# Fixed orders for VectorE, ScalarE and GpSimd, planned at build time from TensorE's order

## The chip, the cores and the metric

One core of a Trainium2 chip. The metric is the device time of one execution in microseconds. Before the change the median of three runs is 2024.77 (2024.56 to 2024.83).

## The reference

Two layers of a decoder trunk, 512 tokens of 1024 numbers, all float32. Cut to what matters:

```python
for l in range(2):
    h = rms_norm(x, gn[0])
    x = x + 0.5 * rms_norm(swiglu(h, w_ffn1_gate[l], w_ffn1_up[l], w_ffn1_down[l]), gn[1])   # D_FF 2816
    h = rms_norm(x, gn[2])
    hq, hf, hi, hg, aq, ak, av, gate_a, gate_b = split(h @ w_in[l])
    y_hg = hgrn2_mixer(hq, hf, hi, hg, ...) @ w_branch_hgrn[l]     # gated linear recurrence, 4 heads, RMS norm for each head
    y_at = swa_sink_attention(aq, ak, av, sinks) @ w_branch_attn[l]  # window 128, 8 heads, softmax with sinks
    x = x + rms_norm((sigmoid(gate_a) * y_hg + sigmoid(gate_b) * y_at) @ w_out[l], gn[3])
    h = rms_norm(x, gn[4])
    x = x + 0.5 * rms_norm(swiglu(h, w_ffn2_gate[l], w_ffn2_up[l], w_ffn2_down[l]), gn[5])
```

## The kernel before

Each large float32 product is three products of fp32r parts: an operand is split into a rounded part `hi` and the rest `lo`, and TensorE computes hi·hi + hi·lo + lo·hi (`mm3`). The split is work for the other engines. ScalarE rounds (`whi`, L288 and L359 for weights, L432 and L442 for activations), VectorE subtracts (`wlo`, L296 and L363; L433), and for some pieces ScalarE writes the negated value (L355, L443) and a GpSimd DMA adds the original onto it (L358, L444).

The FFNs use a scheme with seven products in place of eight. It needs sums and differences of weight quarters (VectorE L340 to L345 into `tt` tiles in the up and gate part, L264 in the down projection), of activations (`quarter_sums`, L490 to L497; for it `Pre.sums`, L595, first adds hi and lo), and of results (L968, L1063 to L1070). After each sub-layer stand two norms for each of four token tiles: squares with a running sum on ScalarE (L639), a root (L644 to L646), the residual step (L863), squares again, and the scaling (L874); then TensorE turns the tile (transposes, L126) and L624 and L630 split it for the next sub-layer.

In the mixer the recurrence's output of each head is normed: Square (L1289), sum (L1291), Sqrt (L1292), reciprocal (L1293), multiply (L1295). The attention beside it takes its exponentials at L1374. ScalarE holds the tables of one set of functions and loads another set where the function needs it (ACT_TABLE_LOAD). PSUM has eight banks, five `acc` and three `aux`; a product into a bank waits until the last reader of the bank's earlier contents is done.

TensorE's order is written out in the program, with coroutines (`Order`, L63) that put small products between the large ones after given delays (`WAIT`). The other engines' orders come from the framework's scheduler, which goes by its own costs; at some 40 places `pin` (`tc.keep_in_program_order`) holds an instruction where the program states it, and `hold` does so in some stretches. Weights come by SyncE's queue in the order of use into four buffers (`w32`), at L244 in four pieces for a 512 KB unit in the down projections, at L247 in one piece elsewhere; at L255 aside into `s` tiles. Each engine runs its own queue strictly in order, so what waits at its head holds back what stands behind.

Of the kernel before, what the change touches and what calls it, by code (L numbers as in the profile page):

```python
# [15 lines left out]
P = 128  # L16
D = 1024
S = 512
# [26 lines left out]

@with_exitstack
def trunk(ctx: ExitStack, tc: tile.TileContext, xin, wall, gains, lbT, hgain, sinks, c_dist, c_mask, c_ident, out):
# [12 lines left out]
    def nm(s):  # L60
        seq[0] += 1
        return f"{s}_{seq[0]}"

    def big(dt=F32, shape=None):
        return sb.tile(shape or [P, S], dt, tag="s", name=nm("s"), bufs=SLOTS)

    def small(shape, tag, bufs=4, dt=F32):
        return sb.tile(shape, dt, tag=tag, name=nm(tag), bufs=bufs)

    def acc():  # L70
        return ps.tile([P, S], F32, tag="acc", name=nm("acc"), bufs=5)

    def aux():
        return ps.tile([P, S], F32, tag="aux", name=nm("aux"), bufs=3)
# [73 lines left out]
    pin = tc.keep_in_program_order  # L148
# [10 lines left out]
    class Stream:  # L159
# [78 lines left out]
        def load(self, upto):  # L238
            while self.dma < min(upto, self.n):
                w = sb.tile([P, D], F32, tag="w32", name=nm("w32"), bufs=W32)  # L240
                u = self.dma
                if isinstance(self.src[u], list):
                    for c, a in self.src[u]:
                        nc.sync.dma_start(w.rearrange("p (m c) -> p m c", m=4) if c is None else w[:, c], a)  # L244
                else:
                    for c in (slice(0, D // 2), slice(D // 2, D)) if u == 0 else (slice(0, D),):
                        nc.sync.dma_start(w[:, c], wall[self.src[u]][:, c])  # L247
                self.raw[u] = w
                self.dma += 1
# [8 lines left out]
        def quarter(self, it):  # L258
# [27 lines left out]
            it.hi, it.lo = (sb.tile([P, D + 64], F32R, tag=t, name=nm(t), bufs=WS)[:, it.at : it.at + D] for t in ("whi", "wlo"))  # L286
# [28 lines left out]
        def hold(self, i):  # L315
            if self.tight:
                pin(i)
# [6 lines left out]
        def split(self):  # L324
# [5 lines left out]
            it.hi, it.lo = (sb.tile([P, D + 64], F32R, tag=t, name=nm(t), bufs=WS)[:, it.at : it.at + D] for t in ("whi", "wlo"))  # L330
# [6 lines left out]
            if it.kind == "b":  # L337

                self.t13 = sb.tile([P, D], F32, tag="tt", name=nm("tt"), bufs=2)
                pin(nc.vector.tensor_tensor(self.t13[:, h[0]], w[:, h[0]], v[:, h[0]], op=ALU.add))  # L340
                pin(nc.vector.tensor_tensor(self.t13[:, h[1]], v[:, h[0]], v[:, h[1]], op=ALU.add))  # L341
                self.t = t = sb.tile([P, D], F32, tag="tt", name=nm("tt"), bufs=2)
# [357 lines left out]
    def down(src, kt, l, n, nxt, fast):  # L700
# [31 lines left out]
        def fetch():  # L732
            g = sb.tile([P, D], F32, tag="tt", name=nm("grow"), bufs=2)
# [302 lines left out]
    def sevenths(pre, between=lambda: None, first=True):  # L1036
# [23 lines left out]
        m = sb.tile([P, 4, H2], F32, tag="m", name=nm("m"), bufs=1)  # L1060
# [82 lines left out]
    class Scores:  # L1143
# [38 lines left out]
        def before(self, b):  # L1182
            self.mv = mv = sb.tile([P, 2 * TT, 96], F32, tag="tt", name=nm("mv"), bufs=2)
# [468 lines left out]
```

## Time and profile before

| what | value |
|---|---|
| profiled execution, its own time | 2024.79 us |
| its span, first to last instruction | 2023.0 us |
| TensorE (PE), share of the span | 100%, 13553 instructions |
| weight loads (PEld) | 89% |
| VectorE (DVE) | 80%, 2894 instructions |
| ScalarE (ACT) | 63%, 2213 instructions |
| GpSimd (POOL) | 13%, 318 instructions |
| moved over the span | 328.07 MB, 162 GB/s |

The busy share of TensorE counts a matmul from its start to a modelled end, so that neighbours overlap; a hole between two matmuls is seen in the list of waits and in the start times of the timeline. A row of the timeline reads: start, duration, engine, line, operation, out<-in, shapes, count, and in brackets the idle time before it with what ended it. Several instructions of one kind in a row are merged, and their duration runs from the first start to the last end.

### The profile page before, as it was taken

How to read it: one execution, taken by the hardware profiler on the slowest of the kernel's cores; microseconds unless marked ns; L12 is line 12 of the kernel's file. 1: busy time of each engine (PE TensorE's matmuls, PEld its weight loads, DVE VectorE, ACT ScalarE, POOL GpSimd, SP SyncE). 2: the span in 40 equal slices, each digit the busy share in tenths (PEclk: the TensorE clock that was granted, in tenths of full speed). 3: DMA queues.
4: the chain of work that ended last, by engine and by line, in shares of the span. 5: the costliest groups of instructions: out<-in, count | busy, mean ns of one | idle time of the engine just before them, and what ended most of it. 6: DMA issues, size and time to landing. Idle time of an engine off the chain costs nothing.

```text
span 2023.0 us, 36425 instructions
## 1 busy us (share of the span) xinstructions
PE 2016.2 (100%) x13553; PEld 1809.1 (89%) x13553; DVE 1624.3 (80%) x2894; ACT 1265.2 (63%) x2213; POOL 268.3 (13%) x318
## 2 busy tenths in 40 slices
PE   9999999999999999999999999999999999999998
PEld 8899988877898999998899998898778989999987
DVE  5888899767786788888998888977686858888888
ACT  7566687447364566658766666864554646666684
POOL 0111140000000011113211111400000100111140
PEclk9999999999999999999999999999999999999999
DMA  8688798311246368879768888872122554788794
GB/s 257 159 193 198 177 203 244 109 63 64 83 104 208 112 158 190 193 189 208 202 170 196 196 190 203 189 223 86 61 74 63 151 182 123 170 193 200 175 202 122
DMA packets 166801, 328.07 MB, mean 162 GB/s; under 512 B 19072, under 2 KB 85088, under 8 KB 166624
## 3 DMA queue, kind: packets, MB, share of 16 engines
q1 hardware_dynamic: 122416, 228.16, 34.1%
q0 software_dynamic: 44064, 97.54, 28.5%
q8 instruction: 106, 1.74, 0.3%
q14 instruction: 71, 0.58, 0.1%
q10 hardware_dynamic: 144, 0.05, 0.0%
HBM read 213.43 MB, written 14.73 MB: 113 GB/s over the span
## 4 chain that ended last, share of the span: by engine, by line
PE 93%; DVE 3%; ACT 1%; DMA 1%; issue 1%; SPq 0%; DVEq 0%; ACTq 0%
PE acc L116 71%; PE aux L116 20%; PE aux L126 2%; DVE wlo L296 1%; DVE s L264 1%; DMA w<-wall 1%; PE acc L126 0%; ACT whi L288 0%; DVE s L968 0%; SPq L244 0%; ACT s L442 0%; ACT s L443 0%; DVE wlo L363 0%; DVE s L863 0%; DVE s L433 0%
## 5 line engine op out<-in xcount | busy, mean ns | idle before, releaser
L116 PE MATMUL acc<-s,whi 128*128 128x256 f32 (+1 forms) x4998 | 1018.9, 303 | 0.0
L116 PEld LDWEIGHTS acc<-s,whi 128*128 128x128 f32 x4998 | 791.5, 188 | 46.6 <-issue 3.2
L116 PE MATMUL acc<-s,wlo 128*128 128x256 f32 (+1 forms) x2488 | 752.5, 302 | 0.1
L116 PEld LDWEIGHTS acc<-s,wlo 128*128 128x128 f32 x2488 | 467.9, 188 | 23.3 <-DVE wlo L363 0.4
L116 PE MATMUL acc<-whi,s 128*128 128x512 f32 x1360 | 441.5, 393 | 0.0
L359 ACT CAST whi<-w 128x1024 fp32r<-128x1024 f32 (+1 forms) x310 | 286.1, 926 | 195.0 <-PE acc L116 124.5
L358 POOL DMA_DIRECT2D wlo<-w x178 | 154.6, 869 | 1200.2 <-ACT wlo L355 715.0
L116 PEld LDWEIGHTS acc<-whi,s 128*128 128x128 f32 x1360 | 255.3, 188 | 57.1 <-issue 3.2
L116 PE MATMUL acc<-wlo,s 128*128 128x512 f32 x680 | 265.5, 390 | 0.2 <-DVE wlo L296 0.2
L355 ACT ACTIVATE wlo<-w 128x1024 fp32r<-128x1024 f32 (+1 forms) x178 | 154.6, 869 | 137.1 <-PE aux L116 98.2
L116 PE MATMUL aux<-s,whi 128*128 128x256 f32 (+1 forms) x1296 | 226.9, 278 | 0.0
L359 ACT CAST whi<-tt 128x1024 fp32r<-128x1024 f32 x160 | 168.4, 1053 | 83.2 <-DVE tt L341 43.0
L363 DVE TENSOR_TENSOR wlo<-w,whi 128x1024 fp32r<-128x1024 f32 (+1 forms) x132 | 157.4, 1205 | 78.3 <-ACT whi L359 78.1
L363 DVE TENSOR_TENSOR wlo<-tt,whi 128x1024 fp32r<-128x1024 f32 x160 | 195.4, 1221 | 9.9 <-ACT whi L359 7.3
L116 PEld LDWEIGHTS aux<-s,whi 128*128 128x128 f32 x1296 | 195.8, 188 | 1.1 <-issue 0.5
L116 PE MATMUL aux<-s,wlo 128*128 128x256 f32 (+1 forms) x648 | 179.8, 277 | 0.0
L116 PEld LDWEIGHTS acc<-wlo,s 128*128 128x128 f32 x680 | 127.8, 188 | 27.0 <-DVE wlo L296 2.1
L116 PE MATMUL aux<-whi,s 128*128 128x512 f32 x432 | 143.7, 390 | 0.0
L444 POOL DMA_DIRECT2D s<-s x128 | 111.1, 967 | 223.5 <-ACT s L432 104.7
L116 PEld LDWEIGHTS aux<-s,wlo 128*128 128x128 f32 x648 | 121.6, 188 | 0.4
L296 DVE TENSOR_TENSOR wlo<-s,whi 128x512 fp32r<-128x512 f32 x160 | 102.7, 686 | 9.9 <-ACT whi L288 9.9
L1070 DVE TENSOR_TENSOR m<-aux,s 128x512 f32<-128x512 f32 x80 | 55.2, 690 | 52.0 <-PE aux L116 51.5
(184 smaller groups left out, 2485.1 us busy)
## 6 DMA issues: line engine op xcount, KB each, us to landing
w<-wall SPq DMA_DIRECT2D x267, 512.0 KB, 3.9
wlo<-w POOLq DMA_DIRECT2D x98, 512.0 KB, 5.4
w<-wall SPq DMA_DIRECT2D x224, 128.0 KB, 3.5
wlo<-w POOLq DMA_DIRECT2D x80, 256.0 KB, 4.2
s<-wall SPq DMA_DIRECT2D x128, 128.0 KB, 4.2
s<-s POOLq DMA_DIRECT2D x64, 256.0 KB, 4.6
x_d<-s SPq DMA_DIRECT2D x48, 256.0 KB, 4.7
s<-x_d SPq DMA_DIRECT2D x48, 256.0 KB, 5.1
```

What stands on the lines that cost most here:

```text
L116: nc.tensor.matmul(o, lhsT, rhs, start=start, stop=stop)
L126: nc.tensor.transpose(o, src, ident)
L264: pin(nc.vector.tensor_tensor(o[c], x[c], y[c], op=op))
L296: pin(nc.vector.tensor_tensor(it.lo[:, h[c]], w[c], it.hi[:, h[c]].bitcast(F32), op=ALU.subtract))
L355: i = nc.scalar.mul(it.lo[:, c], w[:, c], -1.0)
L358: nc.gpsimd.dma_start(it.lo[:, c].bitcast(F32), w[:, c], accum_op=ALU.add)
L359: i = nc.scalar.copy(it.hi[:, c], w[:, c])
L363: self.hold(nc.vector.tensor_tensor(it.lo[:, c], w[:, c], it.hi[:, c].bitcast(F32), op=ALU.subtract))
L444: nc.gpsimd.dma_start(lo.bitcast(F32), src, accum_op=ALU.add)
L1070: ws.hold(nc.vector.tensor_tensor(m[:, 1:3, :], pairs[2], v[:, ::-1, :], op=ALU.add))
```

## The change

All `pin` and `hold` calls become empty, so the program states no order for the three engines any more. At the end of the build `arrange` reads the finished instruction list. `Step` gives every instruction a duration and a time to its result from formulas; `graph` finds the dependences, those through reused buffers too; `ranks` works back from TensorE's order, run without a wait, to the latest time at which each instruction may end; `simulate` runs all queues and on each free engine starts, among what can start soonest (within 0.4 us), the one with the earliest such time. Twelve rounds of this raise the rank of what TensorE waited for, and the round with the earliest end wins. Its orders are fixed by dependences between neighbours. TensorE's order, the DMAs and all arithmetic stay. Tiles are made by one helper, `take`, that also notes the number of buffers; names that were given apart from the tag (`grow`, `mv`) are now `tt`.

```diff
+EARLY_NS, NEAR_NS, TABLE_NS, HOT_NS, SEM_NS = 8000.0, 400.0, 1280.0, 3000.0, 55.0
+ROUNDS = 12
...
+        if op == "InstDMACopy":
+            self.bytes, self.rate = 4 * m * P, 197.0 if i.engine == EN.Pool else 412.0
+            self.cost = 930.0 if i.engine == EN.Pool else 60.0
+            self.time = 2600.0 + self.bytes / self.rate
...
+        elif i.engine == EN.Activation:
+            self.cost = max(0.85 * m + 85.0, 190.0) + (100.0 if len(self.writes) > 1 else 0.0)
+            self.time = self.cost + 100.0 + SEM_NS
+        elif i.engine == EN.DVE:
+            one = op == "InstTensorScalarPtr" and not i.is_scalar_tensor_tensor
+            self.cost = 0.78 * m + 10.0 if one else 1.045 * m + 72.0
+            self.time = self.cost + 78.0 + SEM_NS
...
+def simulate(steps, tags, homes, turn, ideal, rank):
...
+        first = min(x[0] for x in c)
+        near = [x for x in c if x[0] <= first + NEAR_NS]
+        if e == EN.Activation and len(near) > 1:
+            hot = [x for x in near if rank[x[1].n] + lag < x[0] + HOT_NS]
+            near = hot or [x for x in near if x[1].table in (0, table)] or near
+        b = min(near, key=lambda v: (rank[v[1].n], v[1].n))
...
+        for o in s.after:
+            o.left -= 1
+            t = end if o.engine != e or s.bytes else x + s.cost
+            if t >= o.ready:
+                o.ready, o.cause = t, s
...
+    for _ in range(ROUNDS):
+        order = simulate(steps, tags, homes, turn, ideal, rank)
+        end = pe[-1].start
...
+    for l in best[1].values():
+        for a, b in zip(l, l[1:]):
+            tc.add_manual_dep(by[b], a, info, reason="arrange")
...
-    pin = tc.keep_in_program_order
+    def pin(i):
+        return i
...
         def hold(self, i):
-            if self.tight:
-                pin(i)
+            pass
...
+    arrange(nc, tc, homes)
```

Line numbers in the rows of the new orders are those of the new file, 314 or 315 more than before at these places. The number behind a name tells its buffers apart, and in both orders it stands for the same tile.

ScalarE at the head norms of layer 0's recurrence (about 454 us in the span). `s_5263` are the squares, `ss_5265` the sums under the root, `es_5300` and `den_5303` belong to the softmax. Before:

```order
L1289 ACTIVATE s_5263<-aux_5255 128x512
L1292 ACT_TABLE_LOAD
L1292 ACTIVATE ss_5265<-ss_5265,eps_t 128x4
L1369 ACT_TABLE_LOAD
L1369 ACTIVATE es_5300<-es_5300 128x8
L1396 COPY s_5287<-aux_5277 128x512
L1396 COPY s_5288<-aux_5278 128x512
L1374 ACTIVATE s_5187,den_5303<-s_5187,neg_5298 128x256 x2
```

After:

```order
L1603 ACTIVATE s_5263<-aux_5255 128x512
L1688 ACTIVATE s_5187,den_5303<-s_5187,neg_5298 128x256 x2
L1606 ACT_TABLE_LOAD
L1606 ACTIVATE ss_5265<-ss_5265,eps_t 128x4
L1688 ACT_TABLE_LOAD
L1688 ACTIVATE s_5191,den_5303<-s_5191,neg_5298 128x256
L1710 COPY s_5287<-aux_5277 128x512
L1710 COPY s_5288<-aux_5278 128x512
```

The two exponentials (a merged row, x2) that stood behind the copies now stand between the squares and the load of the table that the root needs, and the small exponential on `es_5300` moved away from here.

VectorE at the turn of layer 0's stream out of the mixer (about 693 us). L630 splits the turned tiles, L644, L646, L863 and L874 are the norm chain of the last token tile (`rt_7599` its second root, `s_7603` and `s_7604` its scaled halves), `wlo_7637` and `wlo_7667` are weight splits. Before:

```order
L646 RECIPROCAL rt_7586<-rt_7586 128x1
L863 SCALAR_TENSOR_TENSOR s_7305<-s_7333,rt_7586,s_7305 128x512
L863 SCALAR_TENSOR_TENSOR s_7307<-s_7584,rt_7586,s_7307 128x512
L644 TENSOR_SCALAR rt_7599<-ss_1393_7594 128x1
L646 RECIPROCAL rt_7599<-rt_7599 128x1
L874 TENSOR_SCALAR s_7603<-s_7305,rt_7599 128x512
L874 TENSOR_SCALAR s_7604<-s_7307,rt_7599 128x512
L363 TENSOR_TENSOR wlo_7637<-w_1333_7339,whi_7636 128x1024
L363 TENSOR_TENSOR wlo_7667<-w_1336_7345,whi_7666 128x1024
```

After:

```order
L677 TENSOR_TENSOR wlo_7637<-w_1333_7339,whi_7636 128x1024
L944 SCALAR_TENSOR_TENSOR s_7538<-aux_7532,g_sb,s_7537 128x256
L944 SCALAR_TENSOR_TENSOR s_7541<-aux_7532,g_sb,s_7540 128x256
L677 TENSOR_TENSOR wlo_7667<-w_1336_7345,whi_7666 128x1024
L958 TENSOR_SCALAR rt_7550<-ss_1381_7545 128x1
L958 TENSOR_SCALAR rt_7586<-ss_1322_7318 128x1
L960 RECIPROCAL rt_7550<-rt_7550 128x1
L1188 TENSOR_SCALAR s_7554<-s_7301,rt_7550 128x512
L1188 TENSOR_SCALAR s_7555<-s_7303,rt_7550 128x512
```

The two weight splits that stood behind the last L874 now stand ahead of the whole chain of the norm, whose first two instructions (`rt_7550`, `rt_7586`) follow them.

VectorE in a down projection of layer 0's second FFN (about 948 us). L264 adds weight quarters in `s` tiles, L296 writes the low part that TensorE reads. Before:

```order
L264 TENSOR_TENSOR s_10854<-s_10854,s_10714 128x512
L264 TENSOR_TENSOR s_10855<-s_10855,s_10715 128x512
L296 TENSOR_TENSOR wlo_10864<-s_10821,whi_10863 128x512
L296 TENSOR_TENSOR wlo_10864<-s_10822,whi_10863 128x512
L264 TENSOR_TENSOR s_10821<-w_1844_10376,s_10821 128x512
L264 TENSOR_TENSOR s_10822<-w_1844_10376,s_10822 128x512
L296 TENSOR_TENSOR wlo_10891<-s_10854,whi_10890 128x512
L296 TENSOR_TENSOR wlo_10891<-s_10855,whi_10890 128x512
L264 TENSOR_TENSOR s_10854<-w_1847_10409,s_10854 128x512
```

After:

```order
L611 TENSOR_TENSOR wlo_10864<-s_10821,whi_10863 128x512
L579 TENSOR_TENSOR s_10821<-w_1844_10376,s_10821 128x512
L611 TENSOR_TENSOR wlo_10864<-s_10822,whi_10863 128x512
L579 TENSOR_TENSOR s_10822<-w_1844_10376,s_10822 128x512
L579 TENSOR_TENSOR s_10854<-s_10854,s_10714 128x512
L579 TENSOR_TENSOR s_10621<-s_10621,s_10756 128x512
L579 TENSOR_TENSOR s_10622<-s_10622,s_10757 128x512
L579 TENSOR_TENSOR s_10855<-s_10855,s_10715 128x512
L611 TENSOR_TENSOR wlo_10891<-s_10854,whi_10890 128x512
L611 TENSOR_TENSOR wlo_10891<-s_10855,whi_10890 128x512
```

Two sums on `s_10621` and `s_10622` that ran later now stand ahead of the two halves of `wlo_10891`, and sums and splits alternate where they stood in pairs.

More of the change, by code (lines that the diff above doesn't have):

```diff
@@ L1 @@
+from bisect import bisect_left
 from contextlib import ExitStack
@@ new lines, in place, with graph @@
+def place(a):
+    row = max(a.ap[0][0], 1)
+    part, lo = divmod(a.offset, row)
+    hi = lo + 1
+    for s, c in a.ap[1:]:
+        if s >= 0:
+            hi += s * (c - 1)
+        else:
+            lo += s * (c - 1)
+    return part, part + a.ap[0][1], lo, hi
+def graph(instructions, homes):
+    steps, seen, tags, opener = [], {}, {}, {}
+    for i in instructions:
+        if "Tile" in type(i).__name__:
+            continue
+        s = Step(i, len(steps))
+        steps.append(s)
+        for aps, kind in ((s.reads, 0), (s.writes, 1)):
+            for a in aps:
+                if type(a.tensor).__name__ != "Tile":
+                    continue
+                t = a.tensor.name
+                tag = t.rsplit("_", 2)[0]
+                bank = tag in ("acc", "aux")
+                b = (0, 1, 0, 1) if bank or tag in ("x", "rows") else place(a)
+                log = seen.setdefault(t, ([], []))
+                if tag in homes:
+                    if t not in tags:
+                        tags[t], opener[t] = tag, s
+                        s.opens.append(t)
+                    elif opener[t] is not s:
+                        s.behind[opener[t].n] = opener[t]
+                for o, ob in log[1] + (log[0] if kind or bank else []):
+                    if o is not s and b[0] < ob[1] and ob[0] < b[1] and b[2] < ob[3] and ob[2] < b[3]:
+                        if not (bank and s.engine == EN.PE == o.engine):
+                            s.before[o.n] = o
+                log[kind].append((s, b))
+    for t in tags:
+        for o in {o.n: o for l in seen[t] for o, _ in l}.values():
+            o.closes.append(t)
+    for s in steps:
+        for o in s.before.values():
+            o.after.append(s)
+            s.behind.pop(o.n, None)
+        for o in s.behind.values():
+            o.then.append(s)
+        s.tags = {tags[t] for t in s.opens}
+        s.reads = s.writes = None
+    pe = [s for s in steps if s.engine == EN.PE]
+    for a, b in zip(pe, pe[1:]):
+        if b.wide and not a.wide:
+            a.cost += 100.0
+    return steps, tags
```

233 lines of the change are left out of this document (219 added, 14 removed).

## The prediction

> **What bounds the kernel now.** I read the page's busy times and chain first, then TensorE's own waits, then the timeline at the places where the new orders differ.
>
> ```profile
> span 2023.0 us, 36425 instructions
> PE 2016.2 (100%) x13553; PEld 1809.1 (89%) x13553; DVE 1624.3 (80%) x2894; ACT 1265.2 (63%) x2213; POOL 268.3 (13%) x318
> PE 93%; DVE 3%; ACT 1%; DMA 1%; issue 1%; SPq 0%; DVEq 0%; ACTq 0%
> ```
>
> TensorE is busy from end to end and 93% of the chain is its own matmuls. What it waits for is the list of waits on its engine, whole:
>
> ```profile
> PE aux L116 <- DVE eps_t L139: 1.1, 1, 1.1
> PE acc L126 <- DVE s L863: 1.0, 2, 0.5
> PE acc L116 <- DVE wlo L296: 0.2, 1, 0.2
> ```
>
> Columns are the sum in us, the count and the longest. Of 2.3 us, 1.1 is the start, before any work can be there. So 1.2 us is all that a better order of the other engines can give back (gaps under 0.15 us are not listed). That is 0.06% of the span, and 0.2%, about the least that a measurement of this kernel tells from no change, is 4.0 us. A gain that can be measured is therefore nearly shut out; the question is how many waits the new orders add. TensorE's own order stays, so every new wait on it is lost for good.
>
> **The change part by part.** No instruction is added or removed but one activation table load; GpSimd's order comes out as it was, SyncE's issues shift by a few places. VectorE and ScalarE are reordered nearly everywhere, mostly by a place or two, which TensorE does not see. I price the places where what now stands ahead of something TensorE waits for is longer than the slack that the trace shows there: price = work put ahead, minus slack.
>
> *Place C, the head norms of the recurrence (once a layer).* TensorE's next product into an `aux` bank waits until L1295 has read it.
>
> ```profile
> 454.00 0.60 ACT L1289 ACTIVATE s<-aux 128x512 f32<-128x512 f32 x1 [0.57 <-PE aux L116]
> 454.62 1.28 ACT L1292 ACT_TABLE_LOAD   x1
> 455.92 0.30 ACT L1292 ACTIVATE ss<-ss,eps_t 128x4 f32<-128x4 f32 x1
> ...
> 458.58 0.52 ACT L1374 ACTIVATE s<-s,neg 128x256 f32<-128x256 f32 x1
> ...
> 459.58 0.50 ACT L1374 ACTIVATE s<-s,neg 128x256 f32<-128x256 f32 x1
> ```
> ```profile
> 456.25 0.18 DVE L1293 RECIPROCAL ss<-ss 128x4 f32<-128x4 f32 x1 [0.57 <-ACT ss L1292]
> 456.53 0.69 DVE L1295 TENSOR_TENSOR s<-aux,ss 128x512 f32<-128x512 f32 x1
> ```
> ```profile
> 457.38 0.67 PE L116 MATMUL aux<-s,s 128*128 128x128 f32 x4
> ```
>
> Square, table load, Sqrt, reciprocal and multiply are one chain without a gap; it ends at 457.22, TensorE comes at 457.38: slack 0.16. The new order puts two softmax exponentials between Square and load. Two of them take 1.00 (458.58 to 459.58). 1.00 - 0.16 = 0.84 a layer, 1.7 in all. Bounds: 0 if the exponentials find a hole I do not see, 1.0 each with no slack.
>
> *Place B, the turn out of the mixer (once a layer).*
>
> ```profile
> 693.14 0.88 DVE L874 TENSOR_SCALAR s<-s,rt 128x512 f32<-128x512 f32 x2
> 693.94 2.35 DVE L363 TENSOR_TENSOR wlo<-w,whi 128x1024 fp32r<-128x1024 f32 x2
> ```
> ```profile
> 695.12 0.60 PE L126 MATMUL acc<-ident,s 128*128 128x128 f32 x4
> ```
>
> The second of the four transposes, 0.11 in (695.23), reads what the first L874 wrote, which is done at 693.63 (0.88 for two that overlap, 0.49 for the first): slack 1.60. The two weight splits L363 behind it now stand ahead of the whole chain of the norm; the second begins 1.14 behind the first, so they take 2.28. VectorE has no hole before that chain. 2.28 - 1.60 = 0.68, twice: 1.4 (bounds 0 and 2.28 each).
>
> *Place A, the weight sums in the down projections (four FFNs).*
>
> ```profile
> 947.41 1.29 DVE L296 TENSOR_TENSOR wlo<-s,whi 128x512 fp32r<-128x512 f32 x2
> 948.61 1.29 DVE L264 TENSOR_TENSOR s<-w,s 128x512 f32<-128x512 f32 x2
> ```
> ```profile
> 949.51 0.39 PE L116 MATMUL acc<-wlo,s 128*128 128x512 f32 x1
> ```
>
> The L296 pair ends at 948.70, its second half is read at 949.51: slack 0.81. Two L264 that ran much later now stand ahead: 1.20 (947.41 to 948.61 for a pair of that size). Also, sums and splits now alternate so that each sum waits for the split just ahead. What that costs is in these rows:
>
> ```profile
> 247.46 0.42 DVE L494 TENSOR_TENSOR s<-s 128x256 f32<-128x256 f32 x1
> 247.79 0.42 DVE L491 SCALAR_TENSOR_TENSOR s<-s,s 128x256 f32<-128x256 f32 x1
> 248.25 0.42 DVE L493 TENSOR_TENSOR s<-s,s 128x256 f32<-128x256 f32 x1
> ```
>
> L491 does not need L494 and starts 0.33 behind it; L493 reads what L491 wrote and starts 0.46 behind: 0.13 for a neighbour that is waited for. The planner's list charges nothing for it on one engine. Two such pairs: 0.26. So 1.20 - 0.81 = 0.39, or 0.65 with the pairs; I take 0.5, four times: 2.0 (bounds 0 and 0.65, and 1.46 without slack). The Trainium skill ("VectorE: DVE Perf Modes", section "The DRAIN you can't avoid") says that a semaphore between chained VectorE operations costs nothing extra. By that rule place A is 0.39 and the whole sum 0.4 less; the rows above disagree with it by 0.13.
>
> *Place D, the operand sums before the mixed FFN tiles (three FFNs).*
>
> ```profile
> 712.89 1.29 DVE L433 TENSOR_TENSOR s<-s,s 128x512 fp32r<-128x512 f32 x2 [0.64 <-ACT s L432]
> 715.32 1.29 DVE L1107 TENSOR_TENSOR s<-acc,s 128x512 f32<-128x512 f32 x2 [1.14 <-ACT s L1106]
> ...
> 719.63 1.29 DVE L433 TENSOR_TENSOR s<-s,s 128x512 fp32r<-128x512 f32 x2 [0.23 <-ACT s L432]
> ...
> 723.95 1.29 DVE L433 TENSOR_TENSOR s<-s,s 128x512 fp32r<-128x512 f32 x2 [0.23 <-ACT s L432]
> ```
> ```profile
> 725.88 0.39 PE L116 MATMUL acc<-s,whi 128*128 128x256 f32 x2
> ```
>
> Four weight sums and a split (4 x 0.60 + 1.14 = 3.55, by the pairs above) move ahead of the last L433, whose first half ends at 724.64; its reader is the second of the two at 725.99: slack 1.35. The holes shown add 0.64 + 1.14 + 0.23 + 0.23 = 2.24. 3.55 - 1.35 - 2.24 is just under 0: the cover is those holes, and if the 1.14 is not usable it costs 1.1. I take 0.2, three times: 0.6.
>
> *Place E, the turn into layer 1's mixer (once).*
>
> ```profile
> 1343.35 0.82 ACT L624 ACTIVATE s<-aux,g_sb 128x256 fp32r<-128x256 f32 x2
> 1345.11 0.63 ACT L639 ACTIVATE s<-s 128x512 f32<-128x512 f32 x1 [0.94 <-DVE s L863]
> ...
> 1347.60 1.99 ACT L359 CAST whi<-w 128x1024 fp32r<-128x1024 f32 x2
> ```
> ```profile
> 1347.02 0.16 DVE L646 RECIPROCAL rt<-rt 128x1 f32<-128x1 f32 x1 [0.42 <-ACT rt L645]
> 1347.21 0.88 DVE L874 TENSOR_SCALAR s<-s,rt 128x512 f32<-128x512 f32 x2
> ```
> ```profile
> 1349.30 0.60 PE L126 MATMUL acc<-ident,s 128*128 128x128 f32 x4
> ```
> ```profile
> L247 SPq DMA_DIRECT2D w<-wall x1: 333/333/333, 1337.5 to 1337.5; - x1
> DMA to landing us min/median/max: 8.7/8.7/8.7
> ```
>
> The second of the two casts L359 now stands ahead of the squares L639 on ScalarE. Its weights were asked for at 1337.5 and landed 8.7 later, at 1346.2. So ScalarE would wait for them, cast until 1347.1 (1.99 / 2 each), and start the squares 2.0 later than at 1345.11. On VectorE a split (1.14) now stands ahead of L646, 0.42 of which fits its wait: 0.7. Slack as in place B: 1349.41 - 1347.70 = 1.7. 2.0 + 0.7 - 1.7 = 1.0. Low end 0 if the cast's load comes earlier; high end 2.7 without slack.
>
> *What falls away.* The L863 wait at 2002 (0.5) and the L296 wait at 1995 (0.2): three and ten VectorE instructions that stood ahead of them now stand behind. The second L863 wait, at 2017, keeps its chain. -0.7.
>
> Everything else I cost at nothing: the cover is slack of 1 us and more, as at 258 us in the span, where 1.7 of work moves ahead of a slack of 2.9; if a late load uses that up, up to 1.0 comes on top.
>
> Sum: 1.7 + 1.4 + 2.0 + 0.6 + 1.0 - 0.7 = +6.0. The profiled execution took 2024.79, 1.8 outside its span, and is 0.02 above the median of 2024.77. 2024.8 + 6.0 = 2030.8.
>
> **The rivals.**
> *The covers hold* (ends on the other side: no slower). The same priority that puts work ahead also starts the chains earlier. If it pulls each chain forward by as much as the work put ahead of it, only C remains, since there the chain begins at a matmul's end: 1.7 - 0.7 = +1.0, 2025.8; with C gone too, 2024.1. It decides from 0.8 us of pull at A, 0.7 at B. For it: VectorE idles 20% of the span. Against: at B no hole lies ahead of the chain.
> *Late loads.* The list charges SyncE 0.06 an issue; the trace has
>
> ```profile
> L244 SPq DMA_DIRECT2D w<-wall x272: 327/430/1891, 208.4 to 1977.9; - x136
> ACT whi L288 <- DMA w<-wall: 12.2, 11, 2.2
> ```
>
> 0.43 in the median, and a unit of four pieces is 4 x 0.37 = 1.5 later than planned. ScalarE already waits 11 times for such loads, and in a fixed order the casts behind wait too. If eight such waits (two for each FFN) reach TensorE, +12 on the sum without E: 2024.8 + 5.0 + 12 = 2042. Against: bandwidth, not issue, paces most loads.
> *The change does little:* were the two orders equal where it counts, 2024.8. The rows that moved at A, B and C speak against it.
>
> **How the numbers follow.** Forecast as summed 0.64, covers hold 0.16, late loads 0.16, little 0.04. About 0.10 of the forecast's share lies under 2028.8, where several places come out at their low ends. Faster, that is under 2020.7, would take more than all waits listed and gets 0.03, out of the covers (0.02) and the small change (0.01). Within 0.2%: 0.10 + 0.14 + 0.03 = 0.27. Slower: 0.54 + 0.16 = 0.70. The range reaches down to the covers and up into the late loads, and leaves out about two thirds of these and the faster cases: 2024.2 to 2038.0. The likeliest case alone: 2027 (A, D and E at 0, so -3.6) to 2036 (upper ends of A, D and E, about +5).
>
> **What would show it.** New waits on TensorE's list for VectorE's L1295 (two near 0.8), L874 (three), wlo L296 (four or more), s L433; a ScalarE wait for a `w` load ahead of L639 near 1349; waits at 1995 and 2002 gone; TensorE's busy sum unchanged; direct neighbours on VectorE 0.46 apart more often. Wrong would make it: chains that start earlier than the work put ahead of them costs, or loads that arrive in another order than SyncE's before.

## The result, and the profile after

The changed kernel took 2044.07 us (median of four, 2039.52 to 2048.15), before took 2024.66 (2024.25 to 2024.83): a ratio of 1.0095, interval 1.0083 to 1.0107. It is slower by 19.4 us where +6.0 was forecast, and 2044.07 lies outside the range. Its times also lie 8.6 us apart, where those of before lie 0.6 apart. The profiled execution is the fastest of the four, 2039.52. The page after, its span, busy times and chain:

```profile
span 2037.7 us, 36551 instructions
PE 2025.0 (99%) x13553; PEld 1815.5 (89%) x13553; DVE 1622.9 (80%) x2894; ACT 1256.9 (62%) x2212; POOL 267.4 (13%) x318
PE 84%; issue 6%; DVE 5%; DMA 2%; ACT 2%; SPq 0%; POOL 0%; ACTq 0%; POOLq 0%; DVEq 0%
```

TensorE's list of waits after:

```profile
PE aux L430 <- DVE s L1609: 1.6, 2, 0.8
PE acc L430 <- ACT whi L603: 1.5, 2, 0.9
PE acc L440 <- DVE s L1188: 1.1, 2, 0.6
PE aux L430 <- DVE eps_t L453: 1.1, 1, 1.1
PE acc L430 <- DVE wlo L611: 0.9, 4, 0.2
PE acc L430 <- DVE s L747: 0.8, 2, 0.4
PE aux L430 <- DVE wlo L611: 0.3, 1, 0.3
PE acc L440 <- DVE s L1177: 0.3, 1, 0.3
PE acc L430 <- DMA wlo<-w: 0.2, 1, 0.2
PE aux L430 <- ACT whi L603: 0.2, 1, 0.2
```

The waits came where they were forecast: L1609 is L1295 (place C), L1188 is L874 (B), L611 is L296 (A), L747 is L433 (D). Only the waits for ScalarE's L603 (1.5 and 0.2, at A) were not among those named, and the one of place E is missing. They sum to 8.0 us against 2.3, +5.7. But the span grew by 14.7, and TensorE's busy sum, forecast as unchanged, by 8.8. The list leaves out gaps under 0.15 us; I call these hesitations. Where the busy sum grew is seen in the number of products in stretches of 50 us, first before, then after (columns: stretch, its length, busy us and count of PE, PEld, DVE, ACT, POOL, granted clock, DMA share, GB/s):

```profile
850.00:900.00 50.00, 50.00 (x444) 50.00 (x443) 40.10 (x56) 32.12 (x44) 7.73 (x9) 1.00 0.83 206
```
```profile
850.00:900.00 50.00, 50.00 (x427) 50.00 (x426) 38.44 (x55) 30.00 (x41) 8.60 (x10) 1.00 0.78 185
1850.00:1900.00 50.00, 50.00 (x444) 50.00 (x442) 39.80 (x59) 31.90 (x43) 8.60 (x10) 1.00 0.83 191
```

Busy share and clock are the same in all three rows. Only the count tells: 427 products where there were 444, in the up and gate part of layer 0's second FFN and not in layer 1's. TensorE's timeline after shows where it begins:

```profile
728.93 0.28 PE L430 MATMUL acc<-s,wlo 128*128 128x256 f32 x1
729.04 0.28 PE L430 MATMUL acc<-s,whi 128*128 128x256 f32 x1
729.74 0.39 PE L430 MATMUL acc<-s,whi 128*128 128x256 f32 x1 [0.42 <-DVE s L747]
729.96 0.28 PE L430 MATMUL acc<-s,wlo 128*128 128x256 f32 x1
730.08 0.40 PE L430 MATMUL acc<-s,whi 128*128 128x256 f32 x2
730.31 0.28 PE L430 MATMUL acc<-s,wlo 128*128 128x256 f32 x1
730.43 0.40 PE L430 MATMUL acc<-s,whi 128*128 128x256 f32 x2
730.67 0.28 PE L430 MATMUL acc<-s,wlo 128*128 128x256 f32 x1
```

Ahead of the wait at place D a product of 256 columns starts 0.113 behind the last (0.34 for three). Behind it three take 0.35 to 0.36, and so it stays, at 117.8 ns a product, for 1561 products until the shape changes at 914 us. That costs 6.9 us. I call it the slow rhythm, and such a run of products a slow stretch.

TensorE's order is the same in both kernels, so each product's start can be set against its start before. The lag grows by place as follows (us):

| where | forecast | after |
|---|---|---|
| A, four FFNs, with 0.4 at 258 us and 1.0 at 1257 us | 2.0 | 6.8 |
| B, twice | 1.4 | 1.6 |
| C, twice: the wait itself, 0.95 each | 1.7 | 1.9 |
| C: hesitations of before just ahead of it that are gone | 0 | -1.1 |
| D, three waits (0.70, 0.31, 0.69) | 0.6 | 1.7 |
| ahead of D (701 and 1699 us): products that were slow before and are not, 10 us each time | 0 | -0.8 |
| E | 1.0 | 0 |
| end of the program (1995, 2002, 2017 us) | -0.7 | -1.9 |
| other gains (329, 416, 1328, 1415 us) | 0 | -1.3 |
| a wait for a transfer of GpSimd's (174 us), a hesitation at 1116 us, the start, rest | 0 | 0.9 |
| slow rhythm, 730 to 914 us | 0 | 6.9 |
| sum | 6.0 | 14.7 |

The rows are rounded, and the places are in the times of before. Without the slow rhythm it is +7.8, 2032.6. The table explains the profiled execution, 2039.52. The other three took 3.8 to 8.6 us more and were not profiled; how much of that is further slow stretches is not shown.

### The profile page after: what moved, and what is told of

The parts are those of the page before. It is cut to its first block, busy times and chain, and to the rows that moved or that the text cites. A ratio compares the mean times of both kernels' runs of the same rounds, so it can differ in the third digit from the quotient of the medians.

```text
span 2037.7 us, 36551 instructions
## 1 busy us (share of the span) xinstructions
PE 2025.0 (99%) x13553; PEld 1815.5 (89%) x13553; DVE 1622.9 (80%) x2894; ACT 1256.9 (62%) x2212; POOL 267.4 (13%) x318
## 4 chain that ended last, share of the span: by engine, by line
PE 84%; issue 6%; DVE 5%; DMA 2%; ACT 2%; SPq 0%; POOL 0%; ACTq 0%; POOLq 0%; DVEq 0%
PE acc L430 63%; PE aux L430 19%; PE aux L440 2%; DMA s<-wall 1%; DMA wlo<-w 1%; DVE s L944 1%; DMA w<-wall 1%; ACT whi L603 1%; DVE wlo L611 1%; DVE s L747 1%; DVE wlo L677 1%; DVE s L909 0%; PE acc L440 0%; ACT s L757 0%; SPq L559 0%
## 5 line engine op out<-in xcount | busy, mean ns | idle before, releaser
L1377 DVE TENSOR_TENSOR m<-acc,s 128x512 f32<-128x512 f32 x80 | 55.2, 690 | 119.4 <-PE acc L430 119.4
L611 DVE TENSOR_TENSOR wlo<-s,whi 128x512 fp32r<-128x512 f32 x160 | 100.9, 687 | 12.5 <-ACT whi L603 11.7
```

The source lines that it names most:

```text
L611: pin(nc.vector.tensor_tensor(it.lo[:, h[c]], w[c], it.hi[:, h[c]].bitcast(F32), op=ALU.subtract))
L1377: ws.hold(nc.vector.tensor_tensor(m[:, 0:4:2, :], pairs[0], s.unsqueeze(1).to_broadcast([P, 2, H2]), op=ALU.add))
```

## Experiments: what makes the slow stretch

VectorE's and ScalarE's orders split into 881 and 837 pieces that hold the same instructions before and after. So a kernel was made that takes each engine's order from a list in place of `arrange`, and any piece can be that of before or of after. All other parts are the same. In these kernels line numbers are larger by the length of the lists (300 and a few over those of after); names are unchanged.

**The changed kernel once more** (`again`, no edit).

> The changed kernel, unaltered, once more. Theory R (rhythm): a short wait of TensorE sometimes leaves it in a slower rhythm, 117.8 ns in place of 113.3 for a product of 256 columns, until the next wait or change of shape; the profile of after has it from 730 to 905 us, 6.9 us in all. Which waits do that is chance, so the slow stretch stands elsewhere in this profile, or there are none or two of them, the other differences to before are the same within 0.3 us each (about 7.8 in all), and the times spread over more than 5 us, between 2032 and 2050. Rival O (order): the new orders of the other engines in that stretch slow the products down, by what they read and write meanwhile; then 730 to 905 us is slow again, no other stretch is, and the times lie within 1 us of 2039.5.

2040.33 (2039.63 to 2041.23), ratio 1.0077 (1.0064 to 1.0090). Counts of products in its profile:

```profile
850.00:900.00 50.00, 50.00 (x444) 50.00 (x443) 40.24 (x57) 31.82 (x44) 8.60 (x10) 1.00 0.86 202
1850.00:1900.00 50.00, 50.00 (x427) 50.00 (x426) 38.94 (x58) 30.38 (x42) 8.60 (x10) 1.00 0.82 189
```

The slow stretch has moved to layer 1, behind the wait of place D there, and costs 6.9 again. The same program, other stretch: it is not the order in the stretch. The times of these five lie closer together than expected (1.6 us); with the first four the spread is 8.6. The other differences are not the same within 0.3 us, as they should have been: without the slow stretch it is +9.0, and at A the lag gained at 277 and 288 us, 1.7 and 0.2 in the first profile, is 0.2 and 1.4 here.

**D and the weight passes back** (`both_back`). Place D as before; and in 132 pairs

```diff
-CAST whi_984<-w_139_708 128x512
 ACTIVATE wlo_985<-w_139_708 128x512
+CAST whi_984<-w_139_708 128x512
```

> The new orders with the old one in two things: VectorE and ScalarE ahead of the mixed FFN tiles (place D, three FFNs), and on ScalarE the negated weight before the rounded one, as before, so that GpSimd's transfer starts about 0.95 us earlier (132 pairs). All else is new, VectorE's order in the up and gate stretches too. Theory R: no wait in these stretches, so none of them is slow: 14.7 - 6.9 (slow stretch) - 1.0 (three waits at D) - 0.8 (two waits for GpSimd's transfers, at 174 and 1128 us) = +6.0, 2030.8, and the times agree within 1 us. Rival O: the stretch of layer 0's second FFN is still slow, 2037.8 or more.

2029.64 (2028.18 to 2031.59), ratio 1.0024 (1.0014 to 1.0034). All four long stretches (the up and gate parts of the FFNs) run at 113.3 ns with VectorE's new order in them. The level is 1.2 below the one expected, and the spread of 3.4 us is wider; the waits at A differ between executions (`again`, and below).

**D alone** (`before_d`). On VectorE, for one FFN:

```diff
+TENSOR_TENSOR tt_8018<-w_1405_7640,w_1408_7670 128x512
 TENSOR_TENSOR s_7909<-acc_7610,s_7908 128x512
...
+TENSOR_TENSOR wlo_8017<-tt_8018,whi_8016 128x1024
 TENSOR_TENSOR s_7984<-s_7977,s_7983 128x512
 TENSOR_TENSOR s_7988<-s_7978,s_7987 128x512
-TENSOR_TENSOR tt_8018<-w_1405_7640,w_1408_7670 128x512
...
-TENSOR_TENSOR wlo_8017<-tt_8018,whi_8016 128x1024
```

> The orders of before, with the new ones only at place D (VectorE and ScalarE, 700 to 728, 1030 to 1056 and 1698 to 1727 us). Theory R: three waits, +0.3 each by the traces, 2025.7, and in some executions one, two or three stretches of 175 us behind them in the slow rhythm, about 7 us each: times up to 2047, apart by more than 5 us. Rival O: 2025.7 in every run, since nothing moves in the stretches themselves. If D has no part in it: 2024.8.

2025.68, 2026.22, 2032.02, 2032.21, 2032.44 and 2032.68: two groups, 6.4 apart. In the profile (2032.21) the stretch of layer 1's first FFN is slow, with three waits of 0.3 to 0.5 ahead of the stretches:

```profile
850.00:900.00 50.00, 50.00 (x444) 50.00 (x442) 40.13 (x56) 31.72 (x44) 7.73 (x9) 1.00 0.84 204
1180.00:1230.00 50.00, 50.00 (x427) 50.00 (x426) 39.65 (x55) 29.22 (x39) 7.74 (x9) 1.00 0.82 194
```

**A wait of another origin** (`delay_d`). No new order at all; ahead of the last L433 of place D, in three FFNs:

```diff
+    for _ in range(4):
+        nc.vector.tensor_reduce(pause[:, 32:], pause[:, :32].unsqueeze(2).to_broadcast([P, 32, 16]), axis=AX.X, op=ALU.add)
```

> The orders of before, and on VectorE four idle reductions (0.6 us each, 2.4 in all) ahead of the last L433 before the mixed FFN tiles, in the three FFNs that have place D. None of the new orders is in it. Theory R: three waits of TensorE of 0.5 to 1.1 us (2.4 less the slack of 1.35 and what VectorE makes up), 2026 to 2028, and in some runs one or two stretches of 175 us in the slow rhythm, about 6.9 each: times in two or three groups 6.9 apart. Rival O (the new orders make the slow stretch): 2026 to 2028 in all runs, no slow stretch in the profile.

2028.98, 2029.06, 2029.08, 2029.18, and 2036.12, 2036.38, 2037.28: two groups, 6.9 to 8.3 apart. The profile is of the lower group, and there the waits cost 4.2 (1.3 to 1.5 each, more than expected) and no stretch is slow. So a short wait alone, in the orders of before, is followed by 7 us more in some executions, and no new order is needed for it. That these 7 us are a slow stretch is concluded from their size and from the profile of `before_d`: no execution of the upper group was profiled.

**Delays inside the stretches** (`stalls`, `stalls2`): the same reductions ahead of L1063, 3 to 7 of them in 31 places, then 10 to 18 in 15.

> The orders of before, and 153 idle reductions (0.6 us each by the rows of that size) on VectorE, 3, 5 or 7 in a row ahead of L1063 in every second tile of the four up and gate stretches: 31 delays of 1.8 to 4.2 us that have nothing to do with the new orders. Theory R: TensorE waits at those that exceed its slack of banks, and behind a part of these waits, a fifth to a half, products take 117.8 ns until the next wait; nowhere without a wait ahead. Rival O: waits are added, products stay at 113.3 ns throughout the stretches.

2027.57. TensorE waited in none of the stretches: seven reductions took 4.9 us, and even so VectorE is covered there. Of the 2.8 us that the span is longer than before's, 2.0 came behind two of the stretches, in the down projections (at 257 to 262 and 929 to 933 us). The run says nothing about the rhythm; it suggests that the weak spot of a stretch is its entrance.

> The orders of before, and 10, 14 or 18 idle reductions in a row on VectorE (0.6 us each) ahead of L1063 in every fourth tile of the four up and gate stretches, 15 delays of 6 to 11 us, since 1.8 to 4.2 us had made TensorE wait in none of these stretches. Theory R: TensorE waits at most of them, and behind a fifth to a half of these waits products take 117.8 ns until the next wait or change of shape; before the first wait of a stretch they take 113.3. Rival O: 113.3 behind all of them.

2077.71. TensorE's timeline at one place:

```profile
828.80 0.39 PE L746 MATMUL acc<-s,whi 128*128 128x256 f32 x2
829.14 0.38 PE L746 MATMUL acc<-s,wlo 128*128 128x256 f32 x1
829.36 0.40 PE L746 MATMUL acc<-s,whi 128*128 128x256 f32 x2
829.59 0.28 PE L746 MATMUL acc<-s,wlo 128*128 128x256 f32 x1
829.71 0.40 PE L746 MATMUL acc<-s,whi 128*128 128x256 f32 x2
```

829.14 to 829.36 is 0.22 in place of 0.11; from there three products take 0.35. Of 15 waits in its stretches that 25 or more such products follow, 3 left the slow rhythm, 12 did not, and which it is holds until the next wait or change of shape. With seven other profiles of this study it is 10 of 40, near the lower end of what was expected, and always all or nothing: 113.3 or 117.8, no pace between. At the entrances at place D alone it is 6 of 17. These are waits inside runs of equal products. Behind a change of shape the odds are others: in the trace of before, the ten runs of 29 and 89 such products at the five turns between sub-layers are all slow, and the four long stretches, which follow products of 512 columns, are all at 113.3.

**The exchanged passes** (`d_back`: after with D alone undone; `before_swap`: before with the 132 pairs of the first diff the other way round).

> The new orders with only place D back as before; ScalarE still rounds each weight first and negates it second, so that GpSimd's transfer starts about 0.95 us later than before (the kernel both_back had that undone too and took 2029.6). Theory R: some of these late transfers reach TensorE as waits of 0.1 to 0.4 us (one at 174 us in both profiles of the new kernel, others at 810, 1112 and 1116), at other units from run to run, and a wait sometimes leaves the slow rhythm, up to 7 us for a stretch: times from 2030 to 2040, apart by more than 3 us. Rival: the exchange of the two passes is covered by the transfer's slack and D was the only source of slow stretches: 2029.6 to 2030.4, within 2 us of each other.

2030.93 (2030.24 to 2034.01), ratio 1.0035 (1.0023 to 1.0048). In its profile the lateness at 174 us is there, as a hesitation, and the products behind it, to 234 us, are slow: 2.4 us with the wait. TensorE's list names no transfer.

> The orders of before, ScalarE's two passes over a weight exchanged alone (132 pairs; VectorE as before). Theory R: +0.3 to 0.8 from waits for GpSimd's transfers, and now and then a slow stretch of up to 7 us behind one: 2025 to 2033. Rival, the exchange is covered: 2025.0 in every run, with no wait for a transfer on TensorE's list.

2025.00, ratio 1.0003 (0.9994 to 1.0013), two of 11 runs at 2026.9 and 2027.5. So the exchange is nearly covered, and here the rival came closer than my theory; in `d_back` the spread of 3.8 us and the slow run are as my theory had them. The exchange matters at one unit, sometimes; D makes most of the slow stretches.

## Experiments: the places

**A, B and C alone** (`before_abc`): the new orders of the whole four down projections, of the two turns out of the mixer and of the two mixers, put into the orders of before, such as on ScalarE at C

```diff
 ACTIVATE s_5263<-aux_5255 128x512
+ACTIVATE s_5187,den_5303<-s_5187,neg_5298 128x256 x2
 ACT_TABLE_LOAD
```

> The orders of before, with the new ones only at places A (four down projections), B (two turns out of the mixer) and C (two mixers, 440 to 500 and 1440 to 1502 us). Both theories: the differences of the two traces at these places, 2.3 + 1.0 + 2.5 + 1.0 for A, 0.8 twice for B, 0.4 and 0.5 for C, sum to +9.2: 2034.0, with times that agree within 1 us, since the products behind these waits are of 512 columns or change shape soon. If the waits there come from late weights ahead of the places rather than from the orders at them, 2024.8 to 2027.

2033.64 (2032.99 to 2035.30), ratio 1.0045 (1.0032 to 1.0057). The waits belong to the orders at these places, as expected; which pieces of these orders make them, this run does not tell. At C, ScalarE and then TensorE after:

```profile
455.79 0.60 ACT L1603 ACTIVATE s<-aux 128x512 f32<-128x512 f32 x1 [3.88 <-PE aux L430]
...
457.38 1.28 ACT L1606 ACT_TABLE_LOAD   x1
458.68 0.30 ACT L1606 ACTIVATE ss<-ss,eps_t 128x4 f32<-128x4 f32 x1
```
```profile
458.71 0.40 PE L430 MATMUL acc<-wlo,s 128*128 128x512 f32 x1
458.95 0.40 PE L430 MATMUL acc<-whi,s 128*128 128x512 f32 x1
460.13 1.13 PE L430 MATMUL aux<-s,s 128*128 128x128 f32 x8 [0.78 <-DVE s L1609]
```

The load starts 1.59 behind the square (0.62 before), and TensorE starts 1.18 behind a product, where the one ahead of it took 0.24: 0.95 lost by the starts of the products.

At B, VectorE and TensorE after:

```profile
698.17 0.88 DVE L1188 TENSOR_SCALAR s<-s,rt 128x512 f32<-128x512 f32 x2
```
```profile
698.71 0.55 PE L440 MATMUL acc<-ident,s 128*128 128x128 f32 x3 [0.57 <-DVE s L1188]
```

TensorE is 2.75 us later here than before for what came earlier, and L1188 5.03 later than L874 was: 2.28 for the two splits.

**What makes A cost 6.8.** At A in layer 0's second FFN, ScalarE, VectorE and TensorE after:

```profile
958.13 1.66 ACT L603 CAST whi<-w 128x512 fp32r<-128x512 f32 x3
959.69 0.62 ACT L603 CAST whi<-s 128x512 fp32r<-128x512 f32 x1
```
```profile
960.34 0.69 DVE L611 TENSOR_TENSOR wlo<-s,whi 128x512 fp32r<-128x512 f32 x1 [0.41 <-ACT whi L603]
```
```profile
961.09 0.50 PE L430 MATMUL acc<-wlo,s 128*128 128x512 f32 x1 [0.22 <-DVE wlo L611]
```

The last wait of the second half is not VectorE's own sums: VectorE stands idle 0.41 us until ScalarE has rounded the half, and ScalarE does that behind three casts of later weights. TensorE waits for the rounded half first (0.3 here, 0.2 to 1.0 in the four FFNs), and then 0.50 in each for the low half, whose subtraction can start only behind the cast.

Four kernels start from `both_back`, where A still costs 4.8. In each of the four FFNs the new order had put these three casts on ScalarE, and two early sums on VectorE, between the two halves of one weight sum. `a_cast` moves the cast, `a_sum` the sum, `a_sum_cast` both, `a_late_cast` the cast and both early sums:

```diff
 CAST whi_10890<-s_10854 128x512
+CAST whi_10890<-s_10855 128x512
 CAST whi_10925<-w_1934_10807 128x512 x2
 CAST whi_10951<-w_1939_10840 128x512
-CAST whi_10890<-s_10855 128x512
```
```diff
 TENSOR_TENSOR s_10854<-s_10854,s_10714 128x512
+TENSOR_TENSOR s_10855<-s_10855,s_10715 128x512
 TENSOR_TENSOR s_10621<-s_10621,s_10756 128x512
 TENSOR_TENSOR s_10622<-s_10622,s_10757 128x512
-TENSOR_TENSOR s_10855<-s_10855,s_10715 128x512
```

> The kernel both_back (2029.6; 4.8 us of its difference to before lie at places A) with four rows of ScalarE moved: in each FFN's down projection the second half of a rounded weight sum, which TensorE waits for, moves ahead of three casts of later weights (1.6 us) that the new order had put between the two halves. Nothing else moves on any engine. Theory S (ScalarE's three casts make the waits at A): of the 4.8 us 2.5 to 4 go, and VectorE no longer waits 0.4 us for ScalarE ahead of its second L296: 2025.6 to 2027.3. Rival V (the prediction's step: VectorE's two early weight sums make them): the waits for VectorE stay at 0.4 to 0.5 each, at most 1 us goes: 2028.6 to 2029.6.

2033.41, 3.8 slower than `both_back`, as neither theory had it. ScalarE, and VectorE at the same time:

```profile
277.07 0.62 ACT L903 CAST whi<-s 128x512 fp32r<-128x512 f32 x1 [0.23 <-ACT s L1057]
278.83 0.62 ACT L903 CAST whi<-s 128x512 fp32r<-128x512 f32 x1 [1.14 <-DVE s L879]
```
```profile
276.30 2.49 DVE L879 TENSOR_TENSOR s<-s,s 128x512 f32<-128x512 f32 x4
```

The cast can't start before the fourth of VectorE's sums, two of which are the early ones of the prediction. Moved ahead, it holds ScalarE idle for 1.14, and the casts behind it are late: a unit later TensorE now waits 1.3 in all four FFNs, where in `both_back` it waits 1.0 in two.

> The kernel both_back with four rows of VectorE moved: at each place A the sum of the second half (such as s_10855) ahead of the two early sums (s_10621, s_10622) and not behind them. In a_cast ScalarE's second cast had waited 1.1 us for that sum, and moving the cast alone had cost 3.8. Theory V+S (both engines hold the second half back, VectorE's early sums and ScalarE's three casts): nothing gained here, since the cast stays behind its three neighbours: 2028.8 to 2030. Theory V alone: the waits at A shrink by 0.4 to 0.5 each, 2027.5 to 2028.5.

2029.67 (2027.30 to 2032.05), ratio 1.0022 (1.0013 to 1.0032): nothing gained, as V+S said.

> both_back with the rows of a_cast and of a_sum moved together. Theory V+S: the second half of the low part is ready 0.5 us earlier (VectorE no longer idle 0.4 ahead of it), 1 to 2 us of the 4.8 at A go: 2027.5 to 2028.7, and the extra of a_cast (3.8) is gone since ScalarE no longer stands idle. If A is late for what comes before it (the casts and sums of the unit ahead, late weights): 2029 to 2030.

2028.43 (2026.66 to 2031.60), ratio 1.0018 (1.0009 to 1.0028): the loss of `a_cast` is gone. The median is 1.2 below that of `both_back`, but the two intervals overlap, so a gain is not shown.

> both_back with the prediction's step for place A undone on VectorE (the two early sums behind both halves of the low part) and ScalarE's second cast ahead of the three. Theory V+S: both halves of the low part are ready 1.2 us earlier, the waits at 277, 949, 1276 and 1948 us go (2 to 3 us), 2026.5 to 2027.7; what is left at A is the wait a unit later (1.0 us twice in both_back's profile), which these rows do not touch. If neither engine's order at this spot is the cause: 2029 to 2030.

2029.38 (2027.92 to 2031.65), ratio 1.0022 (1.0013 to 1.0032). In its profile the waits at 277, 949, 1276 and 1948 us are gone, as V+S said; but those a unit later (288, 960, 1287, 1959 us) grew from 2.0 to 4.3, 1.4 came at 258 us, where `both_back` has none, and the time is as without the edit, where the rival had it. Both engines hold the second half back: the rows of after and of `a_cast` show it, and moving the sum alone gains nothing. But A as a whole (4.9 us in the profile of `both_back`, 10.9 in `a_cast`, 8.1 in `a_sum`, 3.4 in `a_sum_cast`, 6.3 in `a_late_cast`) moves from one unit to the next when one is eased, and differs between executions: times of one kernel lie up to 5 us apart, without a slow stretch in the one profile of each. I could not bring it down to one row, and it stays open.

**The planner's list** (`near_priced`, `issue_priced`): after, with one line altered each.

```diff
-            t = end if o.engine != e or s.bytes else x + s.cost
+            t = end
```
```diff
-            self.cost = 930.0 if i.engine == EN.Pool else 60.0
+            self.cost = 930.0 if i.engine == EN.Pool else 430.0
```

> The changed kernel with one line of its planner altered: a result is ready for the same engine as late as for another one, 0.13 to 0.16 us behind the end, which the list of before took as nothing. Theory: part of the waits came from neighbours that the plan took for free (0.13 us each in the trace), so the chains at place D and A are planned earlier; D's three waits go (-1.0), and with them most slow stretches: 2028 to 2033. Rival, the plan goes wrong by other prices and by its choice among what can start, not by this: waits of 7 to 8 us remain, and the time lies at 2032 to 2045 as for the changed kernel.

2053.92 (2052.38 to 2056.22), ratio 1.0143 (1.0130 to 1.0156), far above both expectations. The waits of L747 are gone from the list, but A costs 16.9 (waits for ScalarE's L603, 8.1 in the list), and two stretches are slow, both behind a hesitation too short for the list:

```profile
729.73 0.50 PE L430 MATMUL acc<-s,whi 128*128 128x256 f32 x2
730.06 0.28 PE L430 MATMUL acc<-s,wlo 128*128 128x256 f32 x1
730.18 0.40 PE L430 MATMUL acc<-s,whi 128*128 128x256 f32 x2
730.41 0.28 PE L430 MATMUL acc<-s,wlo 128*128 128x256 f32 x1
```

Two products take 0.33 in place of 0.23, and 0.1 us late becomes 7.0. So charging the neighbour's 0.13 does not mend the plan, and what the plan then orders is worse.

> The changed kernel with one number of its list altered: SyncE's issue of a transfer at 430 ns, the median of the trace, in place of 60. Theory late loads: waits for weights at places A shrink by 2 us or more, 2030 to 2040 with the slow stretches. Rival: late loads have no part in the waits seen (TensorE's list names VectorE and ScalarE), the sum of waits stays at 7 to 9 us, D stays, and the time lies between 2032 and 2048.

2031.34, 2031.92, 2037.88 and 2044.93, which fits none, none, one (in the profile, of 2037.88) and two slow stretches. Ratio 1.0056 (1.0035 to 1.0077). Its median is 2034.90. The waits at A are nearly gone from the list (against 0.9 + 1.5 + 0.3 + 0.2 of after):

```profile
PE acc L430 <- ACT s L846: 1.8, 1, 1.8
...
PE aux L430 <- DVE wlo L611: 0.3, 1, 0.3
...
PE acc L430 <- DVE wlo L611: 0.2, 1, 0.2
```

A falls from 6.8 to 2.6, and a new wait at the start (L846) costs 3.0. So one price in the list, SyncE's 60 for a measured 430 ns, changes A by 4 us in the one profile of each. This one run can't tell whether because the loads themselves come at the planned time, or because the plan came out another way.

**The gains alone** (`gains`, `gains2`): before, with the pieces where after is ahead, such as on VectorE at the end

```diff
 TENSOR_TENSOR s_22799<-acc_22907,s_22799 128x512
-TENSOR_TENSOR s_22800<-acc_22908,s_22800 128x512
 TENSOR_TENSOR wlo_23134<-s_22517,whi_23133 128x512
```

> The orders of before, with the new ones only where the trace of after is ahead: 324 to 352, 405 to 433, 701 to 707, 1322 to 1352, 1405 to 1432, 1698 to 1705 and from 1985 us on. The differences there are -0.3, -0.3, -0.4, -0.4, -0.3, -0.4 and -1.9: -4.0 in all, ratio 0.998, with no slow stretch. If the gains were only lags of earlier places caught up, that is TensorE coming later and so waiting less, 0 to -1.5.

2023.78, ratio 0.9997 (0.9988 to 1.0005). The end keeps -1.7 and 416 and 1415 us keep -0.3 each; the others vanish or, at 324 to 330 us, turn into a loss of 0.6.

> The orders of before, with the new ones only at 405 to 433, 1405 to 1432 and from 1985 us on, the three windows that kept their gain in the profile of the kernel gains (-0.27, -0.28 and -1.7); its other windows gained nothing and cost 0.5 at 277 us. If the gains are the orders' own: -2.2, 2022.6 where before is 2024.8, ratio 0.9989, no new wait on TensorE's list. If they come only where TensorE is late already: 0 to -1.

2023.30, ratio 0.9993 (0.9984 to 1.0002). It is the lowest median of the study, 1.4 below before as measured beside it, and its interval still holds no change. No version here is shown to be faster than before.

## Why the prediction was wrong

- **"TensorE's busy sum unchanged", and each wait priced at its own length.** This step failed, and it is the one that took the time out of the range: the profiled execution is 2039.5 with the slow stretch and 2032.6 without it, and the range ends at 2038.0. A wait at the head of a stretch of 1561 equal products can change their pace by 4% for the rest of it: 6.9 us on top of a wait of 0.3 to 0.7, in a quarter of the waits counted above. The trace of before showed that there are two paces, and I read past it. Behind the turn out of the mixer, at an undisturbed clock, then 23 us later:

```profile
700.70:710.70 10.00, 10.00 (x87) 10.00 (x87) 9.05 (x15) 5.15 (x6) 0.86 (x1) 1.00 0.29 57
724.00:734.00 10.00, 10.00 (x90) 10.00 (x90) 9.90 (x15) 6.98 (x10) 1.72 (x2) 1.00 0.39 98
```

- **The waits without it: +7.8 for a forecast of +6.0,** 2032.6, within the range. The direction and the places were right, also as shown by `before_abc` and `before_d`. That the sum comes so near is luck: by the table, A, B, C, D and the rest were forecast 7.2 too low together, and E and the gains 5.4 too high.
- **C** (0.84 each, 0.95 measured) and **B** (0.68, 0.74) came as worked out. What was missing is the time from the end of the write to TensorE's start, which the sum counted as slack: at C VectorE's L1609 ends at 459.98 and TensorE starts at 460.13, nearly the 0.16 of before; at B it is 0.05 (698.66 to 698.71).
- **A** was mis-sized, 2.0 for a measured 6.8, and the path was wrong too. VectorE's two early sums were named rightly, but not ScalarE's casts beside them, nor that an eased unit hands its lateness on (`a_late_cast`). The wait for the low half, 0.50 in each FFN, has the size that I took, by luck: it is the subtraction behind a late cast, not sums less slack. The waits for the rounded half were not in the sum, nor the 0.11 by which the product behind each wait comes late too (also at D: 729.74 to 729.96 above). My bound of 1.46 for each was too low at two of the four FFNs (2.3 and 2.5); both of these hold the place at 258 us, and the same in layer 1, that was costed at nothing with up to 1.0 for a late load: 0.4 and 1.0 measured, and TensorE's list names ScalarE's L603 and VectorE's L611 there, not a load.
- **D** was mis-sized where it mattered most: 0.2 each, 0.70, 0.31 and 0.69 measured, at the entrance of the long stretches. The holes counted as cover were no cover: after, VectorE's timeline shows no idle time from 711 to 731 us, and L747 still comes late. The 1.1 that was named for the case that a hole is not usable covers all three. (4 x 0.60 + 1.14 is 3.54 and not 3.55, which changes nothing.)
- **E** cost nothing: the cast ran without a wait for its load, the low end that was named. So there were two waits for L874, not three.
- **What falls away**, -0.7, measured -3.2 with the other gains, -1.1 more ahead of C and -0.8 ahead of D. Part of it is not the new orders' own: `before_abc` has the old order at 329 and 1328 us, and there too TensorE, which comes later, gains 0.3 and 0.4.
- **Late loads** as a rival had the time nearly right (2042) and not the mechanism: TensorE's list after names one wait for a transfer, 0.2 us. That SyncE's price was off did matter for A (`issue_priced`).
- **A rule of the Trainium skill that was weighed.** The Trainium skill ("VectorE: DVE Perf Modes", section "The DRAIN you can't avoid") says that a semaphore between chained VectorE operations costs nothing extra. It decided nothing here: charging the 0.13 that the rows show made the plan worse (`near_priced`), and the difference of 0.4 in the sum is lost in the error of A.

## What to carry to other kernels

On an engine that is busy from end to end, price a wait with what it leaves behind, and look for two paces of the same instruction in the trace before you call its busy time fixed: count instructions per stretch, since busy share and clock do not show it. This plan by a list of durations went wrong where the slack was short by a few tenths of a us; keep more slack at the entrance of long uniform stretches than anywhere else. Times of one program that lie in two groups, here 7 us apart, can point to such a pace, and repeating the profile can show where it sits.

## What was not expected of the hardware

- Products of 256 columns, each with its own weight load, keep one of two paces, 113.3 or 117.8 ns, both at clock 1.00 and 100% busy. A wait sets it anew, the slow one in 10 of 40 cases. At the turns between sub-layers, behind a change of shape, the slow one is the rule (ten of ten runs in the trace of before). In the slow one every third weight load has a record of 192 ns for 188. What decides between the two stays open.
- The Trainium skill ("TensorE: Matmul & The Clock Gate", section "Back-to-back issue gap") says that the spacing is set by product and weight load together, and gives an isolated gap that comes to 109 ns here (an estimate by its formula). The trace does not have one spacing for such a pair but two, both above 109 ns; that the weight load is what tells them apart is not shown by any run here.
- A delay of 0.1 us is enough (`near_priced`), and up to 4.9 us of VectorE's delay inside a stretch made TensorE wait nowhere in that stretch (`stalls`).
